# Ordering the weights of a recurrent stage 300 instructions ahead instead of 100, in a hybrid decoder layer

## The chip, the cores and the metric

The kernel runs on one core of one Trainium2 chip. The metric is the device time of one execution in microseconds. Three runs of the kernel before gave 1248.77, 1249.38 and 1249.49 us: median 1249.38. The profile is of one more execution, with its own time.

## The reference, cut to what matters

One decoder layer on 512 tokens of width 1024 in float32: a SwiGLU block, two token mixers side by side (dilated attention and a gated recurrence, RG-LRU) that are merged by gates, and a second SwiGLU block. Root-mean-square norms stand around each. The change is in the recurrent mixer:

```
proj = u @ w_in                       # q, k, v, xr, yr, gl
xc = conv(xr, width 4, causal) + conv_b
gate_x = sigmoid(xc_head @ w_x + b_x);  gate_a = sigmoid(xc_head @ w_a + b_a)   # 4 heads of 256 channels
a = exp(-8 * gate_a * softplus(-a_param))
b = sqrt(1 - a * a) * gate_x * xc
h[t] = a[t] * h[t-1] + b[t]           # a scan over the 512 tokens
rec_d = (h * gelu(yr)) @ w_rec_branch
merged = sigmoid(gl0) * attn_d + sigmoid(gl1) * rec_d
```

## The kernel before

**Products.** Each value is kept as two halves, a high one of reduced precision (float32r) and a low one, the rest. A product is three matmuls for each block of 128 by 128 weights (high by high, high by low, low by high, `mm3`). A part of the weights for one product is 1024 columns wide here (512 in the attention branch). TensorE (PE) runs 24 matmuls of 128 by 512 for each product of a 1024 part: columns of 512 tokens, 8 blocks, three each.

**The weights** are one stream in HBM in the order of their use (`stream_plan`). `raw_of` loads them on SP's DMA queue (L215) in groups of 2048 columns, so two parts of 1024 or four of 512, into tiles `raw`, of which there are two. `split` (L268 to L270) turns a part into its halves, in a tile `w8` (four of them) or, for a part of 512, `w4` (two): ScalarE (ACT) copies the high half (L269), VectorE (DVE) subtracts for the low one (L270). A `raw` buffer is free when all parts of its group are split, a `w8` buffer when the last matmul that reads it is done. `fetch` (L226) does both and stands ahead of each product.

**The order** is made by a planner. Each instruction gets a running number as the code issues it. Inside `tc.high_priority(offset=n)` the numbers go back by n, and what is issued inside takes up no numbers outside. The planner steps through the program with durations of its own: whenever an engine is free there, it gives it the ready instruction with the lowest number, and when a buffer comes free, the waiting instruction with the lowest number gets it. The order that comes out is fixed for each engine and queue; the chip then follows it, each instruction waiting on semaphores for what it needs. `fetch` goes back by `AHEAD` = 100, the evacuations of PSUM by `EVAC` = 200.

**The recurrent stage** (L990 to L1129) follows the attention stage. The attention stage ends with four products by seven sub-products (`seven`, L975 to L980), which take three `w8` and one `w4` each, and eight small products of the attention branch (`fetch(("attn", c))`, L985 to L988: 12 matmuls and one DVE step each, weights in two groups of four parts). Then 31 small steps prepare a constant (L1005 to L1020), and the stage runs its events in the order that was written out by hand (`LRU_ORDER`). h is the head, with two blocks of channels each:

- `conv(h)`: two products; each is copied from PSUM (`xr`, L1037), put through the width-4 convolution (one step on ACT, L1038, three taps on DVE, L1040) and split into `rec.hi[c]`, `rec.lo[c]` (L1042). The first 24 matmuls and one memset of each take numbers; the rest is inside `high_priority(EVAC)`.
- `branch(h)`: two products, copied to `ge` (L1054) and put through GELU (L1060).
- `gates(h)`: one part of weights, four outputs of 6 matmuls each from `rec` of both blocks of the head (L1076 to L1092), each with a sigmoid on ACT (L1090). Of the first output's six matmuls the first three read the head's first block, the fourth `rec.hi` and the fifth `rec.lo` of its second.
- `recur(h)`: 30 steps on ACT and DVE (L1094 to L1120) that make a and b, scan (L1118), multiply with `ge` (L1119) and split the result over `rec` of the same blocks (L1120).
- `gate1(h)`: products for the merge gate (none, two, two and four), copied to `sig` (L1073) and put through a sigmoid (L1066).

The order is conv(0), branch(0), branch(1), conv(1), gates(0) with recur(0), branch(2), conv(2), gates(1) with recur(1), gate1(1), branch(3), gates(2) with recur(2), conv(3), gate1(2), gates(3) with recur(3), gate1(3). It has 28 fetches, 24 matmuls each. After the stage come eight products of `rec` with the recurrent branch's weights (L1133 to L1138), which read all eight blocks of `rec`, block 6 and 7 of head 3 last.

The two lines that decide the order of the stage's weights:

```
with tc.high_priority(offset=ahead if slot else AHEAD):    # fetch, L229
    src = raw_of(key)
```

Of the kernel before, what the change touches and what calls it, by code (L numbers as in the profile page):

```python
# [29 lines left out]
AHEAD = 100  # L30
EVAC = 200
# [102 lines left out]
def stream_groups():  # L134

    groups, cur, w = [], [], 0
    for key, width in stream_plan():
        if w + width > RAW_W or (cur and cur[0][0][0] == "start"):
            groups.append(cur)
            cur, w = [], 0  # L140
        cur.append((key, w, width))
        w += width
    groups.append(cur)
    return groups
# [12 lines left out]
def hybrid_layer(ctx: ExitStack, tc: tile.TileContext, xT: bass.AP, xN: bass.AP, wst: bass.AP,  # L157
# [44 lines left out]


    groups = stream_groups()
    state = {"g": 0, "i": 0, "off": 0, "raw": None}

    def raw_of(key):

        g, i = state["g"], state["i"]
        grp = groups[g]  # L210
        if i == 0:
            w = grp[-1][1] + grp[-1][2]
            raw = wpool.tile([P, RAW_W], F32, name="raw", tag="raw", bufs=2)
            src = bass.AP(tensor=wst.tensor, offset=wst.offset + state["off"], ap=[[w, P], [1, w]])
            nc.sync.dma_start(raw[:, :w], src)  # L215
            state["raw"] = raw
            state["off"] += w * P
        k, o, w = grp[i]
        assert k == key, (k, key)
        src = state["raw"][:, o:o + w]  # L220
        if i + 1 == len(grp):
            state["g"], state["i"] = g + 1, 0
        else:
            state["i"] = i + 1
        return src

    def fetch(key, slot=None, ahead=0):

        with tc.high_priority(offset=ahead if slot else AHEAD):  # L229
            src = raw_of(key)  # L230
            w = src.shape[-1]
            t = slot() if slot else w8() if w > 512 else w4()
            split(t[:, 0, :w], t[:, 1, :w], src)
            return t[:, 0, :w], t[:, 1, :w]

    def w8():
        return wpool.tile([P, 2, 1024], F32R, name="w8", tag="w8", bufs=4)

    def w4():
        return wpool.tile([P, 2, 512], F32R, name="w4", tag="w4", bufs=2)  # L240
# [27 lines left out]
    def split(dh, dl, src):  # L268
        ACT.activation(dh, src, AF.Copy)  # L269
        DVE.tensor_sub(dl, src, dh.bitcast(F32))  # L270
# [7 lines left out]
    def tmp(name):  # L278
        return tpool.tile([P, T], F32, name=name, tag="t")
# [23 lines left out]
    def gemm_first(keys, x, slots, then):  # L303


        wts = [fetch(k, None if i < 4 else slots.pop(0)) for i, k in enumerate(keys)]
        pss = [acc_ps() for _ in keys]
        for sl in HALVES:
            for i, (wt, ps) in enumerate(zip(wts, pss)):
                for k in range(x.n):  # L310
                    mm3(ps[:, sl], k128(wt[0])[:, k, :], k128(wt[1])[:, k, :], x.hi[k][:, sl],
                        x.lo[k][:, sl], k == 0, k == x.n - 1)
                if sl.start == 0:
                    for f in then.get(i + 1, ()):
                        f()
        return pss
# [87 lines left out]
    def last_product(key, nk, x, added, grow, slots, block, fills={}, apart=False):  # L404


        sums = {}
        warm(eps)
        for half, fs in enumerate(FHALVES):
            ws = [fetch(key(half, kk), slots.pop(0) if half else None) for kk in range(nk)]  # L410
            for b in range(4):
                ps = acc_ps()
                tokens(ps, ws, x, b, fills.get((half, b), lambda: None))
                src, y = ps, fb(b, fs)
                if added:
                    DVE.tensor_add(y, ps, y)
                    src = y
                sums[b, half] = square(src)
                z = tmp("z") if apart and half else y
                DVE.tensor_mul(z, src, grow[:, fs])  # L420
                if half:
                    block(b, (sums[b, 0], sums[b, 1]), *([z] if apart else []))
# [201 lines left out]
    def ffn(n, x, r, forms_x, apool, pss):  # L624
# [31 lines left out]
        def down(a, half):  # L656
            ws = [fetch(("down", n, a, half, kk), wd, AHEAD) for kk in range(part_blocks(a))]
            for b in range(4):
                ps, y = acc_ps(), fb(b, FHALVES[half])
                tokens(ps, ws, part(a), b)  # L660
                if a == 0:
                    ACT.activation(y, ps, AF.Copy)
                else:
                    DVE.tensor_add(y, ps, y)
# [67 lines left out]
    for k in range(KC):  # L732
        wh, wl, raw = wts[k]
# [30 lines left out]
    with ExitStack() as mx:  # L764
# [210 lines left out]
        for c in range(0, KC, 2):  # L975
            g, u = tmp("g"), tmp("u")
# [13 lines left out]
    with ExitStack() as mx:  # L990
# [66 lines left out]
        def gelus(hds):  # L1057
            for hd in hds:
                for ge in gels[hd]:
                    ACT.activation(ge, ge, AF.Gelu_apprx_tanh)  # L1060

        def sigmoids():

            while late:
                c = late.pop(0)
                ACT.activation(sig[:, c, :], sig[:, c, :], AF.Sigmoid)  # L1066
# [9 lines left out]
        def gates_of(hd):  # L1076
            wh, wl = fetch(("lru", hd))
            a_ = wh.rearrange("p (w i c) -> p w i c", w=2, i=2)
            b_ = wl.rearrange("p (w i c) -> p w i c", w=2, i=2)
            gs = {}  # L1080
            sigmoids()
            for w, bn in ((1, "ba"), (0, "bx")):
                for j in range(2):
                    ps = aux_ps() if w or not j else acc_ps()
                    for i in range(2):
                        js = slice(j * P, (j + 1) * P)
                        mm3(ps, a_[:, w, i, js], b_[:, w, i, js], rec.hi[2 * hd + i], rec.lo[2 * hd + i],
                            i == 0, i == 1)
                    g = lpool.tile([P, T], F32, name="gt", tag="gt", bufs=6)
                    ACT.activation(g, ps, AF.Sigmoid, bias=col(bn, 2 * hd + j))  # L1090
                    gs[w, j] = g
            return [gs[1, j] for j in range(2)], [gs[0, j] for j in range(2)]  # L1092

        def recur(hd, gel, gas, gxs):  # L1094

            cs = (2 * hd, 2 * hd + 1)
            ths, rs = [tmp("th") for _ in cs], [tmp("r0") for _ in cs]
            for c, th, ga in zip(cs, ths, gas):  # L1100
                ACT.activation(th, ga, AF.Tanh, scale=sp4[:, c:c + 1])
            for c, r0, ga in zip(cs, rs, gas):
                ACT.activation(r0, ga, AF.Exp, scale=sp8[:, c:c + 1])
            for r0, th, ga in zip(rs, ths, gas):
                ACT.activation(r0, r0, AF.Copy, bias=0.5, scale=0.5)
                DVE.scalar_tensor_tensor(ga, th, 1.0, r0, op0=ALU.add, op1=ALU.mult)
                DVE.scalar_tensor_tensor(r0, ga, 2.0, r0, op0=ALU.subtract, op1=ALU.mult)
                DVE.tensor_mul(ga, th, r0)
            for c, gx in zip(cs, gxs):
                DVE.tensor_mul(gx, gx, sig[:, c, :])  # L1110
            for th in ths:
                ACT.activation(th, th, AF.Sqrt)
            for ga in gas:
                ACT.activation(ga, ga, AF.Copy, bias=1.0, scale=2.0)
            for c, r0, th, ga, gx, ge in zip(cs, rs, ths, gas, gxs, gel):
                DVE.scalar_tensor_tensor(th, th, -2.0, r0, op0=ALU.mult, op1=ALU.mult)
                DVE.tensor_mul(gx, gx, th)
                DVE.tensor_tensor_scan(th, ga, gx, 0.0, op0=ALU.mult, op1=ALU.add)  # L1118
                DVE.tensor_mul(pi(ge), ip(th), pi(ge))  # L1119
                split(rec.hi[c], rec.lo[c], ge)  # L1120

        for what, hd in LRU_ORDER:
            if what == "gates":
                recur(hd, gels.pop(hd), *gates_of(hd))
            else:
                {"conv": conv, "branch": branch, "gate1": gate1}[what](hd)
                if what == "branch" and hd % 2:
                    gelus((hd - 1, hd))
        sigmoids()  # L1129
        lpool_cm.__exit__(None, None, None)  # L1130

        mg = act_big("mg")
# [147 lines left out]
```

## Time and profile before

| | |
|---|---|
| median of three runs | 1249.38 us |
| the profiled execution's own time | 1248.34 us |
| its span, from the first to the last instruction | 1246.6 us |
| mean granted clock of TensorE | 0.996 |
| TensorE busy | 1233.0 us (99%) |
| VectorE busy | 928.8 us (75%) |
| ScalarE busy | 663.2 us (53%) |
| loads on SP's queue, of 1024 KB | 110, landing after 4.8 us |

Busy time is what an engine spent in instructions. A timeline row has the start, the duration, engine, line, operation, output and inputs with their shapes, and in brackets how long the engine stood idle before it and what ended that. A row of a view of waits has who waited for whom, the total, how often, and the longest. A row of the windows has a stretch of time, its length, the busy time of each engine (PE, PE's weight loads, DVE, ACT, POOL), the granted clock of PE, the busy share of the DMA engines, and GB/s. A chain that ended last is followed back from the last instruction. All times are us from the span's start.

### The profile page before, as it was taken

Reading aid. Unit: us, or ns where it says so; the run is one execution under the profiler, and the core shown is the slowest. Engines: PE = TensorE matmul, PEld = TensorE weight load, DVE = VectorE, ACT = ScalarE, POOL = GpSimd, SP = SyncE. Lnnn points to the kernel's source line nnn. Section 1 sums busy time; section 2 is a strip of 40 time slices with the busy share of each in tenths; the row PEclk is TensorE's granted clock in tenths of the full one; section 3 lists DMA queues with packets and bytes.
Section 4 is the critical chain, followed back from the end, with each engine's and each line's share of the span. In section 5 each row is a group of like instructions: output and inputs, shape, how many; then the busy total and the mean of one; then the engine's idle time right before and its main releaser. Section 6 shows DMA issues by size and latency. Waiting matters only on the chain.

```text
span 1246.6 us, 19074 instructions
## 1 busy us (share of the span) xinstructions
PE 1233.0 (99%) x7748; PEld 1118.5 (90%) x7748; DVE 928.8 (75%) x1473; ACT 663.2 (53%) x1100; POOL 26.2 (2%) x51
## 2 busy tenths in 40 slices
PE   9999999999999999999999998999999999999997
PEld 8899999999878899999988887888899999999986
DVE  7996777786576588888575888854799667777755
ACT  7555444445355465666533887634565544445432
POOL 0000000000002000000000000000100000000000
PEclk9999999999999999999999999999999999999999
DMA  6322222235414322232342121334443222222241
GB/s 242 106 84 103 104 102 102 103 113 200 170 71 143 102 80 99 77 111 69 123 148 101 68 101 68 135 101 169 136 136 135 102 102 101 102 102 72 101 183 67
DMA packets 27383, 141.37 MB, mean 113 GB/s; under 512 B 2976, under 2 KB 6176, under 8 KB 13216
## 3 DMA queue, kind: packets, MB, share of 16 engines
q1 hardware_dynamic: 20016, 122.86, 27.7%
q0 software_dynamic: 7280, 17.30, 4.0%
q8 instruction: 60, 0.98, 0.3%
q14 instruction: 27, 0.22, 0.1%
HBM read 129.67 MB, written 6.29 MB: 109 GB/s over the span
## 4 chain that ended last, share of the span: by engine, by line
PE 89%; DVE 6%; ACT 3%; issue 1%; DVEq 0%; ACTq 0%
PE acc L594 11%; PE acc L595 11%; PE acc L596 11%; PE acc L388 7%; PE acc L389 7%; PE acc L390 7%; PE acc L282 6%; PE acc L283 6%; PE acc L284 6%; PE aux L595 3%; PE aux L594 3%; PE aux L596 3%; PE acc L793 1%; PE acc L795 1%; PE acc L794 1%
## 5 line engine op out<-in xcount | busy, mean ns | idle before, releaser
L270 DVE TENSOR_TENSOR w<-raw,w 128x1024 fp32r<-128x1024 f32 (+1 forms) x241 | 257.5, 1072 | 97.6 <-ACT w L269 63.5
L269 ACT ACTIVATE w<-raw 128x1024 fp32r<-128x1024 f32 (+1 forms) x241 | 225.0, 937 | 185.7 <-DVE raw L575 60.6
L594 PE MATMUL acc<-big,w 128*128 128x256 f32 x896 | 255.4, 285 | 0.0
L595 PE MATMUL acc<-big,w 128*128 128x256 f32 x896 | 254.4, 284 | 0.0
L596 PE MATMUL acc<-big,w 128*128 128x256 f32 x896 | 254.1, 284 | 0.0
L594 PEld LDWEIGHTS acc<-big,w 128*128 128x128 f32 x896 | 171.6, 192 | 0.9
L595 PEld LDWEIGHTS acc<-big,w 128*128 128x128 f32 x896 | 171.8, 192 | 0.6
L596 PEld LDWEIGHTS acc<-big,w 128*128 128x128 f32 x896 | 171.7, 192 | 0.0
L601 ACT ACTIVATE c<-acc 128x256 f32<-128x256 f32 x172 | 65.2, 379 | 81.8 <-PE acc L596 78.2
L389 PE MATMUL acc<-wd,act 128*128 128x512 f32 x256 | 99.8, 390 | 0.0
L388 PE MATMUL acc<-wd,act 128*128 128x512 f32 x256 | 99.6, 390 | 0.0
L390 PE MATMUL acc<-wd,act 128*128 128x512 f32 x256 | 99.4, 389 | 0.0
L594 PE MATMUL aux<-big,w 128*128 128x256 f32 x288 | 81.5, 283 | 0.0
L595 PE MATMUL aux<-big,w 128*128 128x256 f32 x288 | 81.5, 283 | 0.0
L596 PE MATMUL aux<-big,w 128*128 128x256 f32 x288 | 81.4, 283 | 0.0
L594 PE MATMUL acc<-tx,w 128*128 128x256 f32 x272 | 77.2, 284 | 0.0
L595 PE MATMUL acc<-tx,w 128*128 128x256 f32 x272 | 77.0, 283 | 0.0
L596 PE MATMUL acc<-tx,w 128*128 128x256 f32 x272 | 77.0, 283 | 0.0
L282 PE MATMUL acc<-big,w 128*128 128x512 f32 x192 | 74.7, 389 | 0.0
L283 PE MATMUL acc<-big,w 128*128 128x512 f32 x192 | 74.7, 389 | 0.0
L284 PE MATMUL acc<-big,w 128*128 128x512 f32 x192 | 74.7, 389 | 0.0
L270 DVE TENSOR_TENSOR w<-s,w 128x1024 fp32r<-128x1024 f32 x52 | 63.7, 1224 | 10.1 <-ACT w L269 10.1
(316 smaller groups left out, 2751.3 us busy)
## 6 DMA issues: line engine op xcount, KB each, us to landing
raw<-in_w SPq DMA_DIRECT2D x110, 1024.0 KB, 4.8
big<-act POOLq DMA_DIRECT2D x6, 512.0 KB, 3.3
gains<-in_rows POOLq DMA_DIRECT2D x5, 512.0 KB, 5.1
h<-in_x SPq DMA_DIRECT2D x8, 256.0 KB, 4.8
h<-in_xn POOLq DMA_DIRECT2D x4, 512.0 KB, 7.3
kept_m<-h POOLq DMA_DIRECT2D x4, 512.0 KB, 2.9
h<-kept_m POOLq DMA_DIRECT2D x4, 512.0 KB, 5.8
kept<-h POOLq DMA_DIRECT2D x4, 512.0 KB, 3.3
```

Of the source, the lines that this page charges most:

```text
L269: ACT.activation(dh, src, AF.Copy)
L270: DVE.tensor_sub(dl, src, dh.bitcast(F32))
L282: PE.matmul(ps, wh, xh, start=first, stop=False)
L283: PE.matmul(ps, wh, xl, start=False, stop=False)
L284: PE.matmul(ps, wl, xh, start=False, stop=last)
L388: PE.matmul(ps, x.hi[k][:, bl], wh, start=k == 0, stop=False)
L389: PE.matmul(ps, x.hi[k][:, bl], wl, start=False, stop=False)
L390: PE.matmul(ps, x.lo[k][:, bl], wh, start=False, stop=k == x.n - 1)
L594: PE.matmul(ps, wh, xh, start=start and k == 0, stop=False, skip_group_check=True)
L595: PE.matmul(ps, wh, xl, start=False, stop=False, skip_group_check=True)
L596: PE.matmul(ps, wl, xh, start=False, stop=k == 3, skip_group_check=True)
L601: ACT.activation(c, ps, AF.Copy)
```

## The change

The offset of `fetch` is taken from the state. While the events of the recurrent stage are issued it is `EVAC + AHEAD` = 300; before and after them it is 100, as it was. It covers the 28 fetches of the stage: 14 loads on SP, 28 steps of ACT, 28 of DVE. The fetches of the recurrent branch behind the stage keep 100. No instruction is added or removed, and the numbers of all others stay as they are.

```diff
     groups = stream_groups()
-    state = {"g": 0, "i": 0, "off": 0, "raw": None}
+    state = {"g": 0, "i": 0, "off": 0, "raw": None, "ahead": AHEAD}
...
     def fetch(key, slot=None, ahead=0):
 
-        with tc.high_priority(offset=ahead if slot else AHEAD):
+        with tc.high_priority(offset=ahead if slot else state["ahead"]):
             src = raw_of(key)
...
                 split(rec.hi[c], rec.lo[c], ge)
 
+        state["ahead"] = EVAC + AHEAD
         for what, hd in LRU_ORDER:
             if what == "gates":
                 recur(hd, gels.pop(hd), *gates_of(hd))
...
         sigmoids()
+        state["ahead"] = AHEAD
         lpool_cm.__exit__(None, None, None)
```

## The prediction

> **What bounds the kernel now.** I read the profile's page first: the busy times and the chain that ended last.
>
> ```profile
> span 1246.6 us, 19074 instructions
> PE 1233.0 (99%) x7748; PEld 1118.5 (90%) x7748; DVE 928.8 (75%) x1473; ACT 663.2 (53%) x1100; POOL 26.2 (2%) x51
> ...
> PE 89%; DVE 6%; ACT 3%; issue 1%; DVEq 0%; ACTq 0%
> ```
>
> TensorE (PE) is busy for all but 13.6 us of the span. A change in order can win only where PE stands still or runs slowly, so the list of PE's waits comes next.
>
> ```profile
> PE aux L284 <- DVE w L270: 3.7, 1, 3.7
> PE aux L728 <- DVE eps L201: 1.1, 1, 1.1
> PE aux L448 <- DVE u L440: 0.2, 1, 0.2
> ```
>
> There is one wait of size, and it is on a part of the weights (`w`, split at L270). PE's timeline places it; between the first two rows lie the 24 matmuls of `gates(2)`, between the third and the last those of `gates(3)`.
>
> ```profile
> 740.77 0.39 PE L282 MATMUL aux<-rec,w 128*128 128x512 f32 x1
> ...
> 746.21 0.39 PE L282 MATMUL acc<-big,w 128*128 128x512 f32 x1
> ...
> 767.97 0.39 PE L282 MATMUL aux<-rec,w 128*128 128x512 f32 x1
> 768.20 0.39 PE L283 MATMUL aux<-rec,w 128*128 128x512 f32 x1
> 772.26 0.50 PE L284 MATMUL aux<-rec,w 128*128 128x512 f32 x1 [3.67 <-DVE w L270]
> ...
> 773.31 0.60 PE L282 MATMUL aux<-rec,w 128*128 128x512 f32 x1
> 773.70 0.63 PE L283 MATMUL aux<-rec,w 128*128 128x512 f32 x1
> ...
> 779.03 0.39 PE L282 MATMUL acc<-big,w 128*128 128x512 f32 x1
> ```
>
> `gates(2)` takes 746.21 - 740.77 = 5.44 us, 0.227 a matmul; `gates(3)` takes 11.06. So 5.62 us are lost in one place, and that is **all that the whole stage can give**. 3.83 of them are the wait (the third matmul was due at 768.43, came at 772.26). The other 1.79 follow it: from 773.31 matmuls come 0.4 us apart. The windows show that as a fallen clock, and beside it who is full in this stretch.
>
> ```profile
> 750.00:760.00 10.00, 10.00 (x46) 8.29 (x45) 6.72 (x10) 9.87 (x14) 0.00 (x0) 1.00 0.11 46
> 760.00:770.00 10.00, 8.59 (x38) 6.76 (x37) 10.00 (x15) 6.42 (x9) 0.00 (x0) 1.00 0.01 2
> 770.00:780.00 10.00, 7.74 (x27) 6.20 (x28) 9.94 (x12) 6.25 (x11) 0.00 (x0) 0.83 0.38 118
> ```
>
> After PE and its weight loads the columns are DVE, ACT, POOL, then the clock. ACT is full from 750 to 760 and DVE from 754.6 to 780: two slower engines hold up PE for once, and DVE's order decides what it does first. DVE's timeline:
>
> ```profile
> 754.63 0.69 DVE L1106 SCALAR_TENSOR_TENSOR gt<-th,r 128x512 f32<-128x512 f32 x1 [2.48 <-ACT r L1105]
> ...
> 756.90 1.21 DVE L270 TENSOR_TENSOR w<-raw,w 128x1024 fp32r<-128x1024 f32 x1
> 758.03 0.67 DVE L1108 TENSOR_TENSOR gt<-th,r 128x512 f32<-128x512 f32 x1
> ...
> 761.82 1.06 DVE L1037 COPY xr<-acc 128x512 f32<-128x512 f32 x1
> ...
> 769.80 0.67 DVE L270 TENSOR_TENSOR rec<-sig,rec 128x512 fp32r<-128x512 f32 x1
> ...
> 771.00 1.21 DVE L270 TENSOR_TENSOR w<-raw,w 128x1024 fp32r<-128x1024 f32 x1
> ```
>
> And ACT's, with the first half of the same parts:
>
> ```profile
> 754.51 1.04 ACT L269 ACTIVATE w<-raw 128x1024 fp32r<-128x1024 f32 x1
> 755.46 0.61 ACT L1105 ACTIVATE r<-r 128x512 f32<-128x512 f32 x1
> 755.98 1.04 ACT L269 ACTIVATE w<-raw 128x1024 fp32r<-128x1024 f32 x1
> ```
>
> The split at 771.00 is that of `gates(3)`. Its ACT half is done at 757.02, and its DVE half stands 14 us behind, after the steps of `recur(2)` (L1106 to L1119). The split at 756.90 belongs to the second product of `gate1(2)`.
>
> **The change, part by part.** It adds and removes no instruction: 28 splits (one on ACT, one on DVE each) and 14 loads get numbers that are lower by 200. How much this moves depends on the numbers and on the buffers.
>
> *At `gates(3)`.* Between the first step of `recur(2)` and the fetch of `gates(3)` lie that recurrence's 30 steps, 50 of `conv(3)` and 48 of `gate1(2)`: 128. At 100 ahead the split stands 28 behind the first step, so behind nearly the whole recurrence; at 300 it stands 172 in front of it, and in front of the evacuations of `conv(3)` too. What then holds it is its buffer: four `w8`, so it can start when the product four places earlier, the first of `conv(3)`, is done. That one starts at 746.21 and takes 5.44: 751.65. The part is then there by about 757 and PE no longer waits for it.
>
> What is late next: the fifth matmul of `gates(3)` reads the low half of `rec[7]`, made by `conv(3)`. It would be due at 767.97 + 4 x 0.227 = 768.88; the split at 769.80 ends at 770.47, and with the 0.05 that the row at 772.26 shows behind its releaser that is 770.52. If nothing else moves, a wait of **1.64** is left.
>
> Does `rec[7]` itself move? On DVE the split at 756.90 costs 758.03 - 756.90 = 1.13 and goes forward into the idle 2.48 before 754.63: 1.1 earlier. The split of `gates(3)` takes its place: 1.1 later. The first split of `gate1(3)` (now after 776) also comes into this stretch: up to 1.1 more, but its number is behind those of the `conv(3)` steps, so it mostly takes places between the taps that steps of `recur(2)` fill now. On ACT the half at 754.51 goes in front of the sigmoids of `gates(2)`: 755.46 - 754.51 = 0.95 later for L1105 and with it for L1106. Ends: `rec[7]` 2 us earlier (no wait left) to 2.3 later (wait 3.9, as now). I take 0, as the named pieces nearly cancel.
>
> Does the clock still fall? At the end of the kernel, where PE stops for good, the windows show when it does.
>
> ```profile
> 1238.00:1239.00 1.00, 0.64 (x3) 0.19 (x1) 1.00 (x2) 0.00 (x0) 0.00 (x0) 1.00 0.00 0
> ...
> 1240.00:1241.00 1.00, 0.00 (x0) 0.00 (x0) 0.81 (x4) 0.82 (x3) 0.00 (x0) 0.98 0.97 373
> 1241.00:1242.00 1.00, 0.00 (x0) 0.00 (x0) 0.67 (x4) 0.20 (x1) 0.00 (x0) 0.50 0.01 2
> ```
>
> PE ends at 1238.64 and the clock falls at 1240.96, after 2.3 us of idling; no shorter idling in this trace is followed by a fall. 1.64 is shorter, so I take 0, with 1.79 as the other end. [...]
>
> Sum here: 5.62 - 1.64 = **4.0 us won**.
>
> *At the head of the stage.* The loads move on SP's queue, past the two loads of the attention branch (L985 to L988); no DMA of POOL moves. There the numbers cross. From the first fetch of that branch to that of `conv(0)` lie 8 x 13 steps of the products, 31 small ones (L1005 to L1020) and 3 pool boundaries: 138, fewer than 200. So the loads of `conv(0)` and, 50 further, `branch(0)` now come 62 and 12 in front of the branch's first load, and that of `branch(1)` (236) 16 in front of its second (184). Two `raw` buffers are all there is. What this can cost is read from the timelines of SP, PE, ACT and DVE, and from the view of line L215, which has the time to landing.
>
> ```profile
> 609.54 0.33 SPq L215 DMA_DIRECT2D raw<-in_w  x1
> ...
> 628.37 0.33 SPq L215 DMA_DIRECT2D raw<-in_w  x1
> ...
> DMA to landing us min/median/max: 4.6/4.8/8.5
> ...
> 613.87 0.28 PE L594 MATMUL acc<-tx,w 128*128 128x256 f32 x1
> ...
> 621.07 0.40 PE L282 MATMUL acc<-attn,w 128*128 128x512 f32 x1
> ...
> 631.97 0.39 PE L282 MATMUL acc<-attn,w 128*128 128x512 f32 x1
> ...
> 611.19 0.63 ACT L269 ACTIVATE w<-raw 128x512 fp32r<-128x512 f32 x1 [0.34 <-PE acc L596]
> ...
> 627.66 0.68 DVE L270 TENSOR_TENSOR w<-raw,w 128x512 fp32r<-128x512 f32 x1
> ```
>
> Now the branch's second load goes at 609.54 and the one for `conv(0)` at 628.37. After: these early turns go to `conv(0)` and `branch(0)`; the first buffer is free again when both parts of `conv(0)` are split. These need `w8` buffers that the last seven-product gives up as it runs: one is free before it, the next when its second product is done, at 613.87. With 1.04 and 1.21 for the split that is 616.1; the branch's first load lands 4.8 later, at 620.9, and its first part is whole 0.63 + 0.68 later, at 622.2. Its third matmul is due at 621.07 + 0.45: 0.7 late. The second load can go when the fourth part is split, 628.34 + 0.7 = 629.0, lands at 633.8, is split by 635.1, and is due at 631.97 + 0.7 + 0.45 = 633.1: 2.0 late. Together 2.7 us if PE stands still; 0 if it doesn't, since `conv(0)` is ready and the planner gives a free PE the ready matmul with the lowest number. Its matmuls fill the gap and are only brought forward. I take **0.4**, for what the chip is later than the plan.
>
> *Elsewhere.* The other splits move earlier too, but PE doesn't wait for them; this costs nothing as long as PE has its next parts. At the end of the stage the cover is thin: `rec[7]` of `recur(3)` is split at 800.97 and read by PE at 805.55.
>
> ```profile
> 800.97 0.69 DVE L270 TENSOR_TENSOR rec<-ge,rec 128x512 fp32r<-128x512 f32 x1
> ...
> 805.55 0.39 PE L282 MATMUL acc<-rec,w 128*128 128x512 f32 x1
> ```
>
> That leaves 805.55 - 801.66 = 3.9 us. PE comes 4 us earlier, but `recur(3)` starts from `gates(3)` and comes forward with it. I take 0; if it stayed, 0.1.
>
> Sum: 4.0 - 0.4 = 3.6 us. The profiled execution took 1248.34 us, 1.74 beyond its span: 1244.7. It lies 1.04 under the median 1249.38, so in the median's terms **1245.8 us**.
>
> **Rivals.**
>
> *A, the evacuations of `conv(3)` are pushed back (slower).* For: the split of `gates(3)` now stands in front of them on both engines, which are full there. One such split delays `rec[7]` by up to 1.13 on DVE and 1.04 on ACT; three (the second of `gate1(2)`, `gates(3)`, the first of `gate1(3)`) by 3.4 on DVE alone: `rec[7]` at 773.9, wait 5.0, with the clock 6.8 lost, 1.2 more than now, 1250.6. On both engines, one behind the other, 6.5: 9.9 lost, **1253.7**. From 2.2 us of delay on it is slower than before. Against: one of the three leaves the stretch, one stands behind `conv(3)`. A split can also hold up its queue while its buffer isn't free. In the grouped lines from 640 to 870 ACT's splits stood idle 38.3 us for PE:
>
> ```profile
> L269 ACT ACTIVATE w<-raw 128x1024 fp32r<-128x1024 f32 x42 | 44.2, 1056 | 54.4 <-PE acc L284 38.3 <-issue 7.7 <-DMA raw<-in_w 7.0
> ```
>
> [...] Near `gates(3)` the timeline of ACT shows none of these waits, since PE is ahead there.
>
> *B, the overtaken loads cost PE their full price.* 4.0 - 2.7 = 1.3 won: 1248.1; with both landings at 8.5 instead of 4.8, 7.4 more: 1255.5.
>
> *C, it doesn't do what it says.* If buffers held every split where the numbers don't, nothing would move: 1249.4. Against: the buffer of `gates(3)` is free at 751.65, its DVE half runs at 771.00.
>
> **How the numbers follow.** Forecast 0.58 (own range 1243.5 to 1247.3: no wait left, or 2.1 won), A 0.18, B 0.14, C 0.10. A measurement of this kernel can tell about 0.2% (2.5 us) from no change. Faster by more: the forecast but its last 0.04, 0.54. Slower by more: 0.11 of A, 0.03 of B, 0.14. The rest, 0.32, within. The range 1243.4 to 1251.0 leaves out A's and B's slow ends and 0.03 below.
>
> **What would show it.** Right: PE's wait at `gates(3)` names `rec` (L270) and is under 2.3 us, the clock there stays at 1.00, and the split of `gates(3)` stands before L1106 to L1119 on DVE. On SP the load of `conv(0)` goes by 609.54, and PE mixes matmuls of `conv(0)` among those of the attention branch. Wrong: a wait over 3.8 us at `gates(3)` (A), waits of PE between 621 and 643 (B), or any new wait of over 1 us after 780.

## The result and the profile after

| | before | after |
|---|---|---|
| median of 8 runs each, on one chip | 1249.00 us | 1245.51 us (1244.90 to 1246.55) |
| the profiled execution's own time | 1248.34 us | 1245.37 us |
| its span | 1246.6 us | 1243.6 us |

The ratio is 0.9973, with a 95% interval of 0.9962 to 0.9984. The kernel is 3.5 us faster, and a ratio of 1 lies outside the interval. 1245.8 was predicted.

The page of the kernel after, span and busy times:

```profile
span 1243.6 us, 19076 instructions
...
PE 1232.1 (99%) x7748; PEld 1117.6 (90%) x7748; DVE 930.4 (75%) x1473; ACT 664.3 (53%) x1100; POOL 26.2 (2%) x51
```

The work is the same; PE's idle time fell from 13.6 to 11.5 us. PE's timeline has the place: `gates(3)` runs from the row at 768.51 to the one before 775.89. The row at 621.61 is the first matmul of the attention branch, the last two belong to the first product behind the stage.

```profile
621.61 0.40 PE L282 MATMUL acc<-attn,w 128*128 128x512 f32 x1
...
768.51 0.39 PE L282 MATMUL aux<-rec,w 128*128 128x512 f32 x1
...
770.24 0.50 PE L282 MATMUL aux<-rec,w 128*128 128x512 f32 x1 [0.88 <-ACT rec L269]
771.24 0.50 PE L283 MATMUL aux<-rec,w 128*128 128x512 f32 x1 [0.50 <-DVE rec L270]
771.58 0.40 PE L284 MATMUL aux<-rec,w 128*128 128x512 f32 x1
...
775.89 0.39 PE L282 MATMUL acc<-big,w 128*128 128x512 f32 x1
...
797.65 0.39 PE L282 MATMUL acc<-rec,w 128*128 128x512 f32 x1
...
802.41 0.39 PE L282 MATMUL acc<-rec,w 128*128 128x512 f32 x1
```

The wait of 3.67 for `w` is gone. Two short waits for `rec` stand in its place: the high half of `rec[7]` from ACT, then the low one from DVE. `gates(3)` takes 775.89 - 768.51 = 7.38 us where 5.44 is the least, so 1.94 are lost where 5.62 were: **3.68 us won**. The clock holds, in the windows of the same stretch:

```profile
750.00:760.00 10.00, 10.00 (x46) 8.28 (x45) 6.04 (x8) 9.66 (x13) 0.00 (x0) 1.00 0.21 89
760.00:770.00 10.00, 9.35 (x42) 7.41 (x40) 10.00 (x15) 6.22 (x10) 0.00 (x0) 1.00 0.31 108
770.00:780.00 10.00, 9.26 (x40) 7.45 (x41) 9.97 (x13) 7.68 (x12) 0.00 (x0) 1.00 0.31 105
```

Where the last row had a clock of 0.83 before, it has 1.00. DVE is as full as it was. Only its order is another:

```profile
752.73 1.23 DVE L270 TENSOR_TENSOR w<-raw,w 128x1024 fp32r<-128x1024 f32 x1 [1.48 <-ACT w L269]
...
756.49 0.69 DVE L1106 SCALAR_TENSOR_TENSOR gt<-th,r 128x512 f32<-128x512 f32 x1 [1.93 <-ACT r L1105]
...
758.61 1.21 DVE L270 TENSOR_TENSOR w<-raw,w 128x1024 fp32r<-128x1024 f32 x1
...
765.04 1.23 DVE L270 TENSOR_TENSOR w<-raw,w 128x1024 fp32r<-128x1024 f32 x1
...
769.36 1.23 DVE L270 TENSOR_TENSOR w<-raw,w 128x1024 fp32r<-128x1024 f32 x1
770.50 0.69 DVE L270 TENSOR_TENSOR rec<-sig,rec 128x512 fp32r<-128x512 f32 x1
...
785.07 0.69 DVE L1106 SCALAR_TENSOR_TENSOR gt<-th,r 128x512 f32<-128x512 f32 x1 [1.85 <-ACT r L1105]
...
801.11 0.69 DVE L270 TENSOR_TENSOR rec<-ge,rec 128x512 fp32r<-128x512 f32 x1
```

The rows with `w` are, from above, the splits of the second part of `gate1(2)` (now in the gap ahead of `recur(2)`), of `gates(3)` (758.61, was 771.00), and of the first and second part of `gate1(3)`. `rec[7]` of `conv(3)` is split at 770.50.

The span is shorter by 3.0 and not by 3.68, because this execution was 0.54 late before the change could act: 621.61 against 621.07, with 0.45 of it there by the first L283 of PE (6.79 against 6.34). Such differences of start-up come up between other profiles here too: the same matmul starts at 622.57 in that of E1 below, 1.50 late. So what follows compares stretches, not ends.

### The profile page after: what moved, and what is told of

Same layout as the page of the kernel before. It is cut to its first block, busy times and chain, and to the rows that moved or that the text cites. A ratio compares the mean times of both kernels' runs of the same rounds, so it can differ in the third digit from the quotient of the medians.

```text
span 1243.6 us, 19076 instructions
## 1 busy us (share of the span) xinstructions
PE 1232.1 (99%) x7748; PEld 1117.6 (90%) x7748; DVE 930.4 (75%) x1473; ACT 664.3 (53%) x1100; POOL 26.2 (2%) x51
## 4 chain that ended last, share of the span: by engine, by line
PE 89%; DVE 6%; ACT 4%; issue 1%; DVEq 0%; ACTq 0%
PE acc L594 11%; PE acc L595 11%; PE acc L596 11%; PE acc L388 7%; PE acc L389 7%; PE acc L390 7%; PE acc L282 6%; PE acc L283 6%; PE acc L284 6%; PE aux L595 3%; PE aux L594 3%; PE aux L596 3%; PE acc L793 1%; PE acc L795 1%; PE acc L794 1%
## 5 line engine op out<-in xcount | busy, mean ns | idle before, releaser
L283 PE MATMUL acc<-big,w 128*128 128x512 f32 x192 | 74.7, 389 | 0.0
L284 PE MATMUL acc<-big,w 128*128 128x512 f32 x192 | 74.7, 389 | 0.0
```

The lines of the kernel that those rows point to most:

```text
L283: PE.matmul(ps, wh, xl, start=False, stop=False)
L284: PE.matmul(ps, wl, xh, start=False, stop=last)
```

## The experiments

Theory T: the gain is that one split, of `gates(3)`, leaves the shadow of `recur(2)`; what is left there is the wait for `rec[7]`. Rivals are named at each run. Times are medians, each beside the kernel before on the same chip.

| run | us | before | ratio, 95% interval |
|---|---|---|---|
| E1 `gates(3)` alone | 1244.82 | 1248.62 | 0.9970, 0.9959 to 0.9981 |
| E2 all but `gates(3)` | 1251.75 | 1248.62 | 1.0023, 1.0015 to 1.0032 |
| E3 head of the stage alone | 1248.79 | 1248.62 | 1.0003, 0.9994 to 1.0012 |
| E4 `rec` products too | 1245.72 | 1248.62 | 0.9976, 0.9967 to 0.9985 |
| E7 140 for 300 | 1245.24 | 1250.04 | 0.9966, 0.9954 to 0.9979 |
| E9 two taps less | 1244.91 | 1250.04 | 0.9964, 0.9951 to 0.9976 |
| E5 exchange, 300 | 1244.91 | 1250.04 | 0.9964, 0.9951 to 0.9978 |
| E6 exchange, 100 | 1244.43 | 1250.04 | 0.9964, 0.9951 to 0.9976 |
| E10 exchange, gate_x first, 300 | 1242.81 | 1249.05 | 0.9949, 0.9936 to 0.9961 |
| E11 the same, 100 | 1243.39 | 1249.05 | 0.9955, 0.9942 to 0.9969 |

**E1, one fetch alone.**

```diff
-        state["ahead"] = EVAC + AHEAD
         for what, hd in LRU_ORDER:
+            state["ahead"] = EVAC + AHEAD if (what, hd) == ("gates", 3) else AHEAD
```

> Only the fetch of gates(3) is ordered 300 ahead, the other 27 of the stage stay at 100. Theory T (the gain is this one split leaving the shadow of recur(2)): the DVE half of the split stands near 758 instead of 771.00, the wait of 3.67 us for w at gates(3) goes, the clock stays at 1.00 there, and most of the 3.68 us of the full change is won: 1244.9 to 1246.5. Rival R (the gain is the sum of all splits that come earlier): less than 1.5 us won, 1247.5 or more.

PE's timeline of E1 at `gates(3)`:

```profile
769.48 0.39 PE L282 MATMUL aux<-rec,w 128*128 128x512 f32 x1
...
772.23 0.50 PE L283 MATMUL aux<-rec,w 128*128 128x512 f32 x1 [1.15 <-DVE rec L270]
...
776.88 0.39 PE L282 MATMUL acc<-big,w 128*128 128x512 f32 x1
```

`gates(3)` takes 7.40 us, so 1.96 are lost. That is the whole gain of the change, from one fetch of 28. On DVE its split stands at 758.40 to 760.75 (behind that of `gate1(2)`):

```profile
758.40 2.35 DVE L270 TENSOR_TENSOR w<-raw,w 128x1024 fp32r<-128x1024 f32 x2
```

T holds, and the rival, a sum over many splits, falls.

**E2, all the others.**

```diff
+            state["ahead"] = AHEAD if (what, hd) == ("gates", 3) else EVAC + AHEAD
```

> All fetches of the stage at 300 except that of gates(3), which stays at 100. T: the split of gates(3) stands behind recur(2) as before, and PE waits for it at gates(3): nothing won, 1249 with 1.5 us to either side. R: most is won, 1246 to 1247.

Nothing is won, as T says, but 3.1 us are lost, where T allowed 1.5 to either side. The plan puts the matmuls of `gates(3)` with low weights (L284) behind the first of `gate1(3)`, and then, in PE's timeline:

```profile
777.48 0.79 PE L284 MATMUL aux<-rec,w 128*128 128x512 f32 x1 [5.92 <-DVE w L270]
```

DVE's shows what overtook the split of `gates(3)`, the last row: the two first of `gate1(3)`.

```profile
763.95 1.21 DVE L270 TENSOR_TENSOR w<-raw,w 128x1024 fp32r<-128x1024 f32 x1
...
768.88 1.20 DVE L270 TENSOR_TENSOR w<-raw,w 128x1024 fp32r<-128x1024 f32 x1
...
776.24 1.19 DVE L270 TENSOR_TENSOR w<-raw,w 128x1024 fp32r<-128x1024 f32 x1
```

It comes at 776.24 instead of 771.00. Two splits of 1.13 explain 2.3 of the 5.2; why the plan puts it behind the last scan of `recur(2)` as well wasn't followed up. The clock falls here too: it is 0.79 from 770 to 780 and 0.87 from 780 to 790. What matters is that DVE is full here, busy for all 20 us from 760 to 780, so a place further ahead is taken from someone, and here from the one split that PE waited for.

**E3, the head of the stage.**

```diff
+        for i, (what, hd) in enumerate(LRU_ORDER):
+            state["ahead"] = EVAC + AHEAD if i < 4 else AHEAD
```

> 300 for the first four fetch events alone (conv(0), branch(0), branch(1), conv(1)), 100 for the rest. If the numbers alone decided, the loads of conv(0) and branch(0) would overtake those of the attention branch on SP, and up to 2.7 us would be lost: 1249.4 to 1251.7. If the two raw buffers are handed out in the order in which the code issues their users, the loads keep their order and the stage's head stays as it is: 1249.0, with 0.7 to either side, the load of conv(0) still near 628 us.

As before, within 0.1%. SP's timeline of E3 has the attention branch's second load and that of `conv(0)`:

```profile
610.33 0.33 SPq L215 DMA_DIRECT2D raw<-in_w  x1
...
629.15 0.33 SPq L215 DMA_DIRECT2D raw<-in_w  x1
```

They lie 18.82 us apart; in the kernel before 628.37 - 609.54 = 18.83. The loads didn't change their order, nor in the kernel after.

**E4, the parts behind the stage too.** The offset goes back to 100 only behind the eight products of `rec`.

```diff
         sigmoids()
-        state["ahead"] = AHEAD
...
+        state["ahead"] = AHEAD
```

> As the changed kernel, but 300 also for the eight fetches of the products of rec behind the stage. T with its second bound (DVE and ACT are full to the end of recur(3), whose last split ends only about 0.6 us before PE reads it): their splits come in front of recur(3)'s last steps, push rec[7] back and make PE wait 0.5 to 3 us: 1246 to 1248.5. Rival (the cover there isn't thin): as the changed kernel, 1245.5 with 0.5 to either side.

The mechanism shows and is smaller than expected. PE's timeline:

```profile
802.47 0.50 PE L283 MATMUL acc<-rec,w 128*128 128x512 f32 x1 [0.21 <-DVE rec L270]
```

There is a new wait of 0.21, but no change of time that can be measured. In time the rival is right.

**E7, a step or a slope.**

```diff
-        state["ahead"] = EVAC + AHEAD
+        state["ahead"] = 140
```

> The changed kernel with 140 in the place of 300 for the stage: the split of gates(3) then stands 12 numbers in front of the first step of recur(2), and all splits stay behind the evacuations, which are at 200. T (a step: what counts is on which side of recur(2) the split stands): as the changed kernel, 1245.5 with 0.7 to either side. Rival (a slope, the further ahead the more is won): about a fifth of the gain, 1248 or more.

It is a step: 1245.24, with 1.61 us lost at `gates(3)` (767.94 to 774.99). By their numbers all splits rank behind the evacuations of `conv(3)` again, and no split of `gate1(3)` stands between the taps. `rec[7]` still makes PE wait as long as in E1:

```profile
770.34 0.50 PE L283 MATMUL aux<-rec,w 128*128 128x512 f32 x1 [1.15 <-DVE rec L270]
```

So the two splits of `gate1(3)` are not what keeps `rec[7]` late. Without them steps of `recur(2)` stand between the taps. From the start of `gates(3)` to the split of `rec[7]` it is 769.62 - 767.94 = 1.68 us here and 770.50 - 768.51 = 1.99 in the changed kernel, so they cost 0.3 at most.

**E9, `rec[7]` earlier.** This kernel leaves out two of the four coefficients of the convolution in one block, so it computes something else. It serves to time the wait.

```diff
-                    for t in (2, 1, 0):
+                    for t in ((2, 1, 0) if c < 7 else (2,)):
```

> The changed kernel without two of the three convolution taps of block 7 (so one block of one head is convolved with two coefficients instead of four). On DVE the split of rec[7] in conv(3) then stands four instructions earlier. T (what is left at gates(3), 1.94 us, is the wait for rec[7] alone): gates(3) takes its 5.44 us, the two waits for rec go, 1243.1 to 1244.1. Rival (what is left is in gates(3) itself, or the next part of the weights is late too): gates(3) still takes 6.5 us or more, 1245 or more.

PE's timeline:

```profile
768.51 0.39 PE L282 MATMUL aux<-rec,w 128*128 128x512 f32 x1
...
773.95 0.39 PE L282 MATMUL acc<-big,w 128*128 128x512 f32 x1
...
801.05 0.50 PE L282 MATMUL acc<-rec,w 128*128 128x512 f32 x1 [0.42 <-ACT rec L269]
802.12 0.50 PE L283 MATMUL acc<-rec,w 128*128 128x512 f32 x1 [0.57 <-DVE rec L270]
```

773.95 - 768.51 = 5.44: nothing is lost at `gates(3)`, so `rec[7]` was all that was left there. But most of it is given back 30 us later, where `recur(3)`'s `rec[7]` now comes too late: the time is 1244.91 and not the 1243.1 to 1244.1 that was expected. That is the second bound.

**E5 and E6, `conv(3)` and `branch(3)` exchanged**, at 300 and at 100; the GELUs of the last two branches then follow each branch.

```diff
-             ("gates", 1), ("gate1", 1), ("branch", 3), ("gates", 2), ("conv", 3), ("gate1", 2), ("gates", 3),
+             ("gates", 1), ("gate1", 1), ("conv", 3), ("gates", 2), ("branch", 3), ("gate1", 2), ("gates", 3),
...
-                if what == "branch" and hd % 2:
-                    gelus((hd - 1, hd))
+                if what == "branch" and hd:
+                    gelus((0, 1) if hd == 1 else (hd,))
```

> The changed kernel with conv(3) and branch(3) changed places in the order of events, so that rec[6] and rec[7] are made 7 products before gates(3) reads them. T: nothing is lost at gates(3) and 1.94 us more are won, 1243.1 to 1244.1, unless recur(3), whose last split stands 0.6 us in front of PE's reading, now makes PE wait for the same time: then 1244.5 to 1245.5 with a wait of PE for rec at the products behind the stage. Rival (the new place makes another wait of 2 us or more in the stage): 1246 or more.

> The kernel before, all fetches at 100, with the same exchange of conv(3) and branch(3). The steps of conv(3), 7.6 us of DVE, leave the stretch of recur(2) and gates(3). T (the split of gates(3) was late because DVE had more to do in front of it than fits): the wait goes without the change, 1243.5 to 1245. Rival (the number 100 alone keeps the split behind recur(2), whatever else stands there): the wait for w stays over 2 us, 1247 or more.

PE's timeline of E5:

```profile
768.00 0.39 PE L282 MATMUL aux<-rec,w 128*128 128x512 f32 x1
...
773.44 0.39 PE L282 MATMUL acc<-big,w 128*128 128x512 f32 x1
...
799.28 0.39 PE L282 MATMUL acc<-rec,w 128*128 128x512 f32 x1
800.71 0.50 PE L283 MATMUL acc<-rec,w 128*128 128x512 f32 x1 [1.04 <-DVE rec L270]
```

Again 5.44 at `gates(3)`, and again a wait behind the stage, 800.71 - 799.28 - 0.23 = 1.20 late. E6 gets to the same time without the change. DVE, relieved of `conv(3)`, splits `gates(3)`'s part at 763.55, and `gates(3)` starts at 769.72. The first row is from DVE's timeline of E6, the second from PE's:

```profile
763.55 1.21 DVE L270 TENSOR_TENSOR w<-raw,w 128x1024 fp32r<-128x1024 f32 x1
...
769.72 0.39 PE L282 MATMUL aux<-rec,w 128*128 128x512 f32 x1
```

The place in the numbers does not decide alone. What counts is whether DVE gets there in time. The rival of E6 falls.

What holds `recur(3)`? ACT's timeline of E5, from the third of its four sigmoids on:

```profile
777.98 0.67 ACT L1090 ACTIVATE gt<-aux,first 128x512 f32<-128x512 f32 x1
778.66 1.28 ACT L1103 ACT_TABLE_LOAD   x1
779.96 0.73 ACT L1103 ACTIVATE r<-gt,sp 128x512 f32<-128x512 f32 x1
...
781.65 1.28 ACT L1090 ACT_TABLE_LOAD   x1
782.95 0.69 ACT L1090 ACTIVATE gt<-acc,first 128x512 f32<-128x512 f32 x1
783.66 1.28 ACT L1103 ACT_TABLE_LOAD   x1
784.95 0.73 ACT L1103 ACTIVATE r<-gt,sp 128x512 f32<-128x512 f32 x1
```

The first Exp goes ahead of the fourth sigmoid, which costs two more table loads of 1.28 us on the way of `recur(3)`. This is E5's case, and not that of every run: E6 and E9 have one such load in this place (782.19 and 782.15), and their matmuls behind the stage come 1.2 to 1.5 us late all the same. (In E6 the two extra loads stand one head earlier, at 755.30 and 757.30.) The fourth sigmoid belongs to gate_x, which the recurrence needs last; so gate_x goes first:

**E10 and E11, the exchange and gate_x first**, at 300 and at 100.

```diff
-            for w, bn in ((1, "ba"), (0, "bx")):
+            for w, bn in ((0, "bx"), (1, "ba")):
                 for j in range(2):
-                    ps = aux_ps() if w or not j else acc_ps()
+                    ps = aux_ps() if not w or not j else acc_ps()
```

> The exchange of conv(3) and branch(3) at 300 ahead, and in each gates(h) the two outputs of gate_x ahead of those of gate_a, so that the recurrence's Exp steps come behind all four sigmoids. T (what is lost at 800 is recur(3)'s chain on ACT, which in the exchanged kernel loads the tables of Exp and sigmoid twice, 2 x 1.28 us, between its first and its second Exp): PE's wait of 1.04 us for rec behind the stage goes, nothing is lost at gates(3), span 1.2 us shorter than with the exchange alone, time 1243 to 1244.5. Rival (gate_a coming 2.7 us later eats it, or DVE is the limit): a wait of 0.8 us or more stays, 1244.5 to 1246.

> The same with all fetches at 100, so without the change. T: as the run at 300, 1243 to 1244.5, no wait of PE over 0.5 us between 640 and 830. Rival (without the change the split of gates(3) is late again): a wait for w of 1 us or more, 1245 or more.

ACT's timeline of E10:

```profile
779.86 1.28 ACT L1103 ACT_TABLE_LOAD   x1
781.16 1.34 ACT L1103 ACTIVATE r<-gt,sp 128x512 f32<-128x512 f32 x2
```

Both Exp steps are done at 782.5 instead of 785.7. These are all of PE's waits in E10:

```profile
PE aux L728 <- DVE eps L201: 1.1, 1, 1.1
PE aux L448 <- DVE u L440: 0.2, 1, 0.2
```

No wait is left in the stage. 1242.81 us is 6.2 us below before and the lowest of all; PE is busy without a gap from 640 to 830. How much of this is due to the table loads and how much to the other moves that come with the new order was not separated. E11 has the same waits, and is as fast within the intervals. With this order the change brings nothing that can be measured: the 5.62 us could be had from either side.

## Why the prediction was right

**The ceiling of 5.62 us**: right. Where nothing is lost in the stage any more (E10), the first matmul behind it comes 800.79 - 795.07 = 5.72 us earlier than in the kernel before, of which 0.11 are start-up (620.96 against 621.07), so 5.61. The two rows, of before and of E10:

```profile
800.79 0.39 PE L282 MATMUL acc<-rec,w 128*128 128x512 f32 x1
...
795.07 0.39 PE L282 MATMUL acc<-rec,w 128*128 128x512 f32 x1
```

**The split of `gates(3)` goes from behind `recur(2)` to its front**: right, 758.61 for 771.00. E1 shows that it alone carries the gain, E2 that the others without it gain nothing.

**A wait of 1.64 for `rec[7]` stays**: right in its cause (E9), 0.3 too small. The fifth matmul was due at 768.51 + 4 x 0.227 = 769.42 and came at 771.24, 1.82 late; the next came 0.34 behind it, 0.11 more than the pitch. `rec[7]` on DVE did stay where it was: 770.50 - 0.54 against 769.80, 0.16 later where 0 was taken, out of -2 to +2.3. Of the reasons given, the one on `gate1(3)` holds: its splits (two, where one was named) came in and took places that steps of `recur(2)` had. E7, which has them behind, gets `rec[7]` 0.3 earlier and no more. What fills the gaps between the taps is whatever is ready.

**The clock stays up**: right. With waits of up to 1.15 us at `gates(3)` (E1, E7) it is 1.00 in every window from 740 to 810, with those of 3.67 (before) and 5.92 (E2) it falls, to a mean of 0.83 and 0.79 from 770 to 780. Waits between these didn't come up, so what one of them does in the stage was not shown. The time since PE stopped does not fix it alone: the clock fell 2.3 us after that at the end of the kernel, but 4.7 us after it in the stage (from 768.20 + 0.39 to 773.31), when PE was already running again.

**The head of the stage, 0.4 us**: wrong, in its mechanism. It said that the loads of `conv(0)` and `branch(0)` overtake those of the attention branch, because their numbers are lower. They didn't (E3), and PE mixed no matmuls. The two `raw` tiles are given out as if in the order in which the code asks for them, whatever the number: the kernel's description above, that the lowest number gets the buffer, doesn't hold for these loads. The runs fit this: numbers order instructions that are ready on one engine, and a load whose buffer belongs to an earlier one isn't ready. So rival B had no ground.

**`recur(3)` comes forward with `gates(3)`**: wrong. Its first step on DVE behind the Exp (L1106) stands at 785.07 in the kernel after. In DVE's timeline of the kernel before it is

```profile
784.95 0.69 DVE L1106 SCALAR_TENSOR_TENSOR gt<-th,r 128x512 f32<-128x512 f32 x1 [1.94 <-ACT r L1105]
```

so that with the 0.54 of start-up it came 0.4 forward, and PE 3.7. The price is paid by `recur(2)`. Its steps gave their places on DVE to the splits, and its last multiplication starts 3.0 us later than before, with the start-up taken off. DVE's rows, of before and after:

```profile
775.05 1.08 DVE L1119 TENSOR_TENSOR ge<-th,ge 128x512 f32<-128x512 f32 x1
...
778.60 1.07 DVE L1119 TENSOR_TENSOR ge<-th,ge 128x512 f32<-128x512 f32 x1
```

ACT copies the two results of `recur(2)` at 777.47 and 779.70, in between the sigmoids of `gates(3)`, and waits for each of them (0.69 and 0.41 us). The first Exp of `recur(3)` behind these sigmoids starts at 783.17, where it started at 783.06 before. The cover (the time from the end of its split to PE's reading) of `rec[7]`, 3.9 us before, is now 802.41 - (801.11 + 0.69) = 0.6. That was the other end named in the prediction (0.1 if it stayed), and so it cost nothing here; but with so little cover E5, E6 and E9, which win the last 1.94 at `gates(3)`, give 1.2 to 1.5 of it back.

**The sum**: 4.0 - 0.4 = 3.6 predicted, 3.68 measured at `gates(3)`. The wait was 0.3 larger, the head cost 0.4 less: two errors that nearly cancel, so that the sum comes this close is in part luck. Rival A didn't come: DVE's splits ahead of `rec[7]` took the places of steps of `recur(2)`, not of the taps.

## What to carry to other kernels

Look for the one instruction that the bounding engine waits for, and move that one (E1); moving all of its kind gave no more, and moving all but it lost 3.1 us (E2). When a wait goes, the engine that was late may still be as full, so compute the cover at its next meeting point with the bounding engine: here 3.9 us fell to 0.6, and most of what was won beyond that was lost again 30 us later, until the order of the gates was changed as well (E10). In this planner a priority orders what is ready, and, as E3 suggests, it doesn't give an instruction a buffer that is promised to an earlier one.

## What was not expected of the hardware

The prediction has no term for a switch of ACT's table. In E5 one took hardly more than its load of 1.28 us: the load at 778.66 starts 0.01 behind the end of the sigmoid at 777.98, and the Exp follows 0.02 behind the end of the load, so 1.31 us lie between the two steps.
